# Five small moves in the RG-LRU stage of a hybrid streaming layer: the convolution's first tap, the fp16 hi halves, two buffer rings, and the place of the background work

## The chip, the cores and the metric

The kernel runs on one core of a Trainium2 chip. The metric is the device time of one execution in microseconds (us), the median of several runs. A core has five engines with a queue each: TensorE (PE, matmuls), VectorE (DVE), ScalarE (ACT), GpSimd (POOL) and SyncE (SP), which here issues nearly all DMAs. An engine runs its queue in order; semaphores order the engines against each other.

## The reference, cut to what matters

One layer is applied to 2048 prompt positions and to 32 sample positions (with cached keys and values of 512 positions). Both go through the same code, cut here to the path that the change touches:

```
z = rms_norm(x, norm_g) @ w_in                 # 1024 -> 6 x 512
xl, gl, q, k, v, ga = split(z)
xc = conv_b + sum(xl[t-3+k] * conv_w[k] for k in 0..3)      # causal, per channel
r  = sigmoid(xc @ gate_a_w + gate_a_b)         # 8 blocks of 64x64
i  = sigmoid(xc @ gate_x_w + gate_x_b)
a  = exp(-8 * r * softplus(-lambda))
h  = scan(h*a + sqrt(1-a*a) * (i*xc))          # over positions
lru = h * silu(gl)
att = banded attention of q, k, v * silu(ga)   # with the cache for the sample
h  = x + [lru, att] @ w_out
y  = h + (p @ w_pe) * sigmoid(rms_norm(h) @ w_pg)
```

The matmuls take fp16 pairs: each operand is scaled by a power of two and split into a hi half (rounded to fp16) and a lo half (the rest), and three of the four products are summed. The scale comes from a bound on the operand, the largest absolute value.

## The kernel before, in words

The kernel has a front part (about the first 640 us) and an attention part. In the front part the weights `w_in` are loaded and split, `proj(i, b)` (line 265 and on) computes one 128-row tile of q, k, v or the attention gate with 24 matmuls of 128x512, and `POST[b](i)` turns it into fp16 halves in DRAM. The RG-LRU path works on chunks of 256 positions: `l_proj(c, g)` (lines 575 to 616) computes 128 channels of `xl` and `gl` of chunk `c` with 48 matmuls of 128x256 (line 587). After them ACT writes `xl` (L600) and a sigmoid (L603), POOL makes the first tap of the convolution with its bias (L611), and DVE adds the other three taps (L614). `l_split` (lines 618 to 627) makes the halves `X`: ACT the two hi halves of 64 partitions each (L624), DVE the two lo halves (L625). `l_gates(c, g)` runs four small matmuls on `X` (L641) into one of two PSUM buffers of the pool `ps_g`, and ACT reads them with four sigmoids (L644, L645), which frees the buffer. `l_tail(c)` holds the exponentials, the square root and the scan, `l_halves(c)` the bound and the halves of the result.

`l_steps(c)` is a generator that yields between these calls. The loop (`for c in range(2, NCH - 2)`, line 810 and on) has a block per `proj`: a block takes two steps of `l_steps(c - 1)`, a `proj`, one step of the chunk before, and three or four steps of `background()`. A chunk has eight blocks; in the first four stands an `l_proj`. The background does what is not bound to a position: the bias rows (`ext_row`, `ext_store`), the cached keys and values, and the loading, bounding and splitting of `w_out`, `w_ple_gate` and `w_ple_proj` for the attention part. Its `pause` entries are steps that do nothing, between the loads of an operand and its bound. What is left of it after the loop is run at once after four more blocks (`for _ in bg: pass`).

A bound is a maximum over all partitions, `all_max` (lines 82 to 91): DVE puts each partition's maximum on the diagonal of `dg` (L87, one buffer), a matmul with ones spreads it (L90), and DVE reduces it (L91). This bound product takes a buffer of the same pool `ps_g` as the gates, and it is held behind the last matmul that was written down before it:

```
ps = ps_g.tile([128, 2, CW], F32, tag="g", name="psm").rearrange("p a b -> p (a b)")[:, :128]
with tc.issue_after(after.ins) if after else nullcontext():
    nc.tensor.matmul(ps, lhsT=ones, rhs=dg, start=True, stop=True)
```

The order of each engine's queue is set before the run by a planner that takes, of the instructions that are ready by its own estimate of time, the one written first. An instruction without such a hold can so stand in its queue ahead of work that is written before it.

`split(hi, lo, src, s)` (lines 155 to 163) makes the hi half on POOL (L158) or ACT (L160) and the lo half on DVE (L163). `v_half` (lines 406 to 412) splits 128 rows of the cached v into the tile `vTo`, which has one buffer and serves also `post_v` (lines 318 to 327), the v of the prompt (stored by L327). The tile `hlA` is a ring of two, used by the background's weights. `split` of the tokens is in `prep_x(i)` (L223 on ACT, then POOL and DVE, then the transposing DMA L234). `load_x`/`prep_x(SAMPLE)` stand in the first block of the chunk loop with `c == SP` (3), the four sample projections in its blocks 4 to 7.

Of the kernel before, what the change touches and what calls it, by code (L numbers as in the profile page):

```python
# [8 lines left out]
F32 = mybir.dt.float32  # L9
F16 = mybir.dt.float16  # L10
BF16 = mybir.dt.bfloat16
U32 = mybir.dt.uint32
AF = mybir.ActivationFunctionType
OP = mybir.AluOpType
# [20 lines left out]
def hybrid_layer(  # L35
# [313 lines left out]
    def background():  # L349
# [55 lines left out]

        def v_half(j, d):
            def f(st):
                t = Tp("vTo", [128, 2, 512], F16, 1)
                split(t[:, 0], t[:, 1], st[:, d], sV)
                nc.sync.dma_start(kc_d[2 * j + d][:, 1], t.rearrange("p a b -> p (a b)"))  # L410
            return f
# [51 lines left out]
        def load(st, src):  # L463
            nc.sync.dma_start(flat(st) if len(src.shape) == 2 else st, src)

        pause = [(None, ())] * 4
        items = [(None, (ext_load,))] + pause + [(None, (ext_row,))] + pause
        for src, factors, half in ((cache_k, k_factors, k_half), (cache_v, v_factors, v_half)):
            items += [(cache(src, j), (part_max(j),)) for j in range(2)] + pause
# [105 lines left out]
    def l_proj(c, g):  # L575
        n = width(c)
        pt = ps_x.tile([128, 2, CW], F32, tag="x", name="psx")
        for j in range(2):
            i = 0
            for k in range(8):  # L580
                for a, e in ((0, 0), (0, 1), (1, 0)):
                    if c == SAMPLE:
                        rhs, o = xT_s[:, e * 8 + k], pt[:, j, :n]
                    else:
                        rhs = xT[c][:, :, e * 8 + k, :]
                        o = pt[:, j].rearrange("p (a b) -> p a b", a=2)
                    m = nc.tensor.matmul(o, lhsT=wl[j][:, k, a, g * 128:(g + 1) * 128], rhs=rhs, start=i == 0, stop=i == 23)  # L587
                    i += 1
        last_mm[:] = [m]
        if g == 0:  # L590
            b = "s" if c == SAMPLE else ""
            C[c] = {k: TL(k + b, [128, 4, n if b else CW], F32, nb) for k, nb in (("i4", 1 if b else 2), ("sl4", 1 if b else 2))}
        xl = TL("xl", [128, CW + 3])
        if c == 0:
            nc.vector.memset(xl[:, 0:3], 0.0)
        elif c == SAMPLE:
            nc.vector.tensor_copy(xl[:, 0:3], col[:, SCV + 3 * g:SCV + 3 * g + 3])
        else:
            nc.vector.tensor_copy(xl[:, 0:3], hist[g])
        nc.scalar.activation(xl[:, 3:3 + n], pt[:, 0, :n], AF.Copy, scale=u_xl)  # L600
        z = C[c]["sl4"][:, g, :n]
        zs = TL("zs", [128, CW])[:, :n]
        nc.scalar.activation(zs, pt[:, 1, :n], AF.Sigmoid, scale=u_gl)  # L603
        nc.vector.scalar_tensor_tensor(z, pt[:, 1, :n], u_gl, zs, op0=OP.mult, op1=OP.mult)
        hb = small[:, (16 if c == SAMPLE else 0) + 3 * g:][:, :3] if c in (SAMPLE, NCH - 1) else \
            sm.tile([128, 3], F32, tag=f"hist{g}", name=f"hist{g}")
        nc.vector.tensor_copy(hb, xl[:, n:n + 3])
        if c != SAMPLE:
            hist[g] = hb
        xc = C[c]["i4"][:, g, :n]  # L610
        nc.gpsimd.tensor_scalar(xc, xl[:, 0:n], col[:, CWT + g:CWT + g + 1], col[:, CB + g:CB + g + 1],  # L611
                                op0=OP.mult, op1=OP.add)
        for k in range(1, 4):
            nc.vector.scalar_tensor_tensor(xc, xl[:, k:k + n], col[:, CWT + 4 * k + g:CWT + 4 * k + g + 1],  # L614
                                           xc, op0=OP.mult, op1=OP.add)
        l_split(c, g)

    def l_split(c, g):
        n = width(c)
        xc = C[c]["i4"][:, g, :n]  # L620
        X = TL("Xs", [128, 2, NS], F16, 4) if c == SAMPLE else TL("X", [128, 2, CW], F16, 4)
        for o in range(2):
            q, w = slice(o * 64, o * 64 + 64), slice((1 - o) * 64, (2 - o) * 64)
            nc.scalar.activation(X[q, o, :n], xc[q], AF.Copy, scale=sx[q, g:g + 1])  # L624
            nc.vector.scalar_tensor_tensor(X[w, o, :n], xc[q], sx[q, g:g + 1], X[q, o, :n], op0=OP.mult,  # L625
                                           op1=OP.subtract)
        xs_l[c, g] = X
# [154 lines left out]
    prep_w_in(3, stg[3])  # L782
    es_lt.close()
    lt.append(pool("lt", stack=esl))
    ls = l_steps(0)
    for i, b in ((3, 2), (0, 3), (1, 3), (2, 3), (3, 3)):
        next(ls)
        proj(i, b)
        next(ls)
    lp = None  # L790


    bg = background()

    def x_pair(n, c):

# [13 lines left out]
    for c in range(2, NCH - 2):  # L810
        steps = [(i, b) for i in (2 * c, 2 * c + 1) for b in (1, 0, 2, 3)]
        lp, ls = ls, l_steps(c - 1)
        for n, (i, b) in enumerate(steps):
            next(ls, None)
            proj(i, b)
            next(ls, None)
            next(lp, None)
            if c == 2:
                next(lp, None)
            for _ in range(4 if n % 3 == 0 else 3):  # L820
                next(bg, None)
            if c == SP and n == 0:
                load_x(SAMPLE)
                prep_x(SAMPLE)
            if c == SP and 4 <= n < 8:
                proj(SAMPLE, (1, 0, 2, 3)[n - 4])
            if c == SP + 1:
                next(lss, None)
                next(lss, None)
            x_pair(n, c + 1)  # L830
    c = NCH - 2

    def dense(lp, ls, steps):
# [467 lines left out]
```

## Time and profile before

| | before |
|---|---|
| median of 3 runs | 1241.63 us (1239.91 to 1242.02) |
| profiled execution: its own time / its span | 1243.85 us / 1241.9 us |
| PE busy | 1083.4 us (87%) |
| DVE / ACT / POOL busy | 828.2 (67%) / 609.7 (49%) / 451.0 us (36%) |
| mean granted TensorE clock | 0.943 of full |

The span runs from the first to the last instruction of the profiled execution. Busy time of PE is that of matmuls, whose ends are modelled. In a timeline row, the bracket at the end is the time for which the engine sat idle before the instruction, and what ended it.

### The profile page before, as it was taken

The page shows a single profiled execution, that of the slowest core. Times are in us where ns is not written, and L with a number is a line of the kernel's source. Part 1 is how long each engine was busy: PE and PEld are TensorE (multiplying, and loading weights), DVE is VectorE, ACT ScalarE, POOL GpSimd, SP SyncE. Part 2 cuts the span into 40 slices and gives each one's busy share as a digit, 9 for nine tenths or more (in the row PEclk, how much of TensorE's full clock was granted, in tenths as well). Part 3 has the DMA queues.
Part 4 walks back from the last instruction along what each step waited for, and adds up shares of the span by engine and source line. Part 5 has one row for each costly group of instructions (what it writes and reads, how often), then busy time and mean ns, then how long its engine had stood idle before and what let it go on. Part 6 is the DMA issues. An engine that isn't in the chain of part 4 may idle for free. (4 is left out here: it accounts for less than half of the span.)

```text
span 1241.9 us, 22414 instructions
## 1 busy us (share of the span) xinstructions
PE 1083.4 (87%) x8395; PEld 628.6 (51%) x8395; DVE 828.2 (67%) x1860; ACT 609.7 (49%) x1076; POOL 451.0 (36%) x518
## 2 busy tenths in 40 slices
PE   3779998976799789877988689999999999999896
PEld 1335664643465546555634445555555555555443
DVE  5986455844967756776855676667776776676544
ACT  6532565536557755448654254444444444444223
POOL 2875124424546334563420222222222222222221
PEclk9889999997899899978988699999999999999998
DMA  8775313689386684640598988899989899999841
GB/s 290 212 194 170 81 59 73 173 235 269 95 234 164 192 225 149 195 127 26 151 341 269 217 152 163 183 186 198 199 183 183 189 188 186 181 189 187 189 82 26
DMA packets 357725, 217.47 MB, mean 175 GB/s; under 512 B 296032, under 2 KB 298632, under 8 KB 357488
## 3 DMA queue, kind: packets, MB, share of 16 engines
q1 hardware_dynamic: 357184, 215.50, 71.9%
q8 instruction: 65, 1.06, 0.4%
q10 hardware_dynamic: 432, 0.54, 0.1%
q14 instruction: 44, 0.36, 0.1%
HBM read 98.87 MB, written 46.76 MB: 117 GB/s over the span
## 5 line engine op out<-in xcount | busy, mean ns | idle before, releaser
L183 PE MATMUL psp<-wA,xT 128*128 128x512 f16 x1536 | 363.5, 396 | 22.3 <-DVE t L308 9.4
L183 PEld LDWEIGHTS <-xT 128*128 128x128 f16 x1536 | 154.2, 101 | 237.7 <-issue 62.3
L994 ACT ACTIVATE S<-S,nb,s 128x640 f32<-128x640 f32 (+5 forms) x130 | 110.5, 850 | 222.9 <-DVE nb L991 214.4
L183 PE MATMUL psg<-g,hT 128*128 128x512 f16 (+1 forms) x792 | 180.8, 377 | 3.2 <-DVE gt L189 1.5
L587 PE MATMUL psx<-xT,wl 128*128 128x256 f16 x1536 | 181.2, 279 | 0.0
L587 PEld LDWEIGHTS <-wl 128*128 128x128 f16 x1728 | 158.8, 100 | 38.1 <-issue 13.3
L1010 DVE TENSOR_TENSOR Phl<-S,Phl 128x640 f16<-128x640 f32 (+4 forms) x126 | 97.8, 780 | 89.9 <-POOL Phl L1007 48.0
L1032 PE MATMUL pso<-kv,PT 128*128 128x64 f16 (+1 forms) x1704 | 117.1, 195 | 29.0 <-DVE att L1068 16.2
L1032 PEld LDWEIGHTS <-PT 128*128 128x128 f16 (+2 forms) x1800 | 109.7, 99 | 52.1 <-issue 21.4
L1007 POOL TENSOR_SCALAR Phl<-S 128x640 f16<-128x640 f32 (+4 forms) x63 | 48.6, 771 | 211.9 <-ACT S L994 171.3
L977 PE MATMUL pss<-kv,qT 128*128 128x128 f16 (+2 forms) x1200 | 108.1, 223 | 9.1 <-DVE mx L988 7.5
L183 PEld LDWEIGHTS <-hT 128*128 128x128 f16 x792 | 73.9, 99 | 79.5 <-issue 4.3
L977 PEld LDWEIGHTS <-qT 128*128 128x128 f16 (+1 forms) x1200 | 94.8, 100 | 21.2 <-issue 8.2
L988 DVE CUSTOM_DVE_ANT_0 S<-pss,bias 128x640 f32<-128x640 f32 (+4 forms) x128 | 92.9, 731 | 4.5 <-PE pss L977 4.0
L183 PE MATMUL psu<-o,AT 128*128 128x512 f16 x384 | 90.6, 387 | 0.9 <-DMA AT<-An 0.7
L183 PE MATMUL psu<-o,L 128*128 128x512 f16 x384 | 90.4, 386 | 0.2 <-DVE ga L337 0.2
L624 ACT ACTIVATE X<-i,sx 64x256 f16<-64x256 f32 x64 | 32.2, 504 | 75.9 <-DVE i L614 75.1
L1148 POOL TENSOR_TENSOR gt<-gt,h 128x512 f32<-128x512 f32 (+1 forms) x32 | 41.7, 1304 | 65.6 <-DVE gt L1147 58.5
L90 PE MATMUL psm<-dg,ones 128*128 128x128 bf16 x25 | 6.0, 239 | 66.8 <-DVE dg L87 37.5
L96 POOL TENSOR_TENSOR fh<-fh,pw 128x8 f32<-128x8 f32 (+1 forms) x34 | 58.5, 1721 | 2.2
L95 POOL TENSOR_SCALAR fh<-ssqh,e 128x8 f32<-128x8 f32 (+1 forms) x34 | 17.4, 511 | 112.3 <-DVE ssqh L282 79.1
L183 PEld LDWEIGHTS <-AT 128*128 128x128 f16 x384 | 36.4, 100 | 42.4 <-issue 4.6
(284 smaller groups left out, 1716.4 us busy)
## 6 DMA issues: line engine op xcount, KB each, us to landing
stw<-in_w_in_dram SPq DMA_DIRECT2D x20, 512.0 KB, 6.4
x<-in_x_prompt_dram SPq DMA_DIRECT2D x16, 512.0 KB, 4.4
stg<-in_w_out_dram SPq DMA_DIRECT2D x16, 512.0 KB, 5.1
stg<-in_w_ple_gate_dram SPq DMA_DIRECT2D x16, 512.0 KB, 4.6
qT<-qd SPq DMA_DIRECT2D x32, 256.0 KB, 5.5
kv<-kvd SPq DMA_DIRECT2D x16, 512.0 KB, 4.3
h<-in_x_prompt_dram SPq DMA_DIRECT2D x16, 512.0 KB, 4.9
out_dram<-gt SPq DMA_DIRECT2D x31, 256.0 KB, 2.3
```

Source lines behind the costliest of these rows:

```text
L95: nc.gpsimd.tensor_scalar(dst, ssq, mul, add, op0=OP.mult, op1=OP.add)
L96: nc.gpsimd.tensor_tensor(dst, dst, pw[:R, :n], op=OP.pow)
L183: m = nc.tensor.matmul(ps[:R], lhsT=l(a), rhs=r(e), start=first and j == 0, stop=last and j == 2)
L587: m = nc.tensor.matmul(o, lhsT=wl[j][:, k, a, g * 128:(g + 1) * 128], rhs=rhs, start=i == 0, stop=i == 23)
L624: nc.scalar.activation(X[q, o, :n], xc[q], AF.Copy, scale=sx[q, g:g + 1])
L977: last_mm[0] = nc.tensor.matmul(ps[rw, c], lhsT=q[:, h % 2, a * 4 + h // 2, :R], rhs=k[:, h, :n], start=a == 0, stop=a == 1)
L988: nc.vector.tensor_tensor_reduce(out=S[:, c0:c0 + W], in0=ps[:, c0:c0 + W], in1=bias[:, h, 640 - W:], op0=OP.add, op1=OP.max, scale=1.0, s ...
L994: nc.scalar.activation(S[:, c0:c0 + W], S[:, c0:c0 + W], AF.Exp, bias=nb[:, j:j + 1], scale=scP, accum_out=sums[i][:, e:e + 1])
L1007: nc.gpsimd.tensor_scalar(v[:, 0, :W], P[:, :W], 1.0, 1.0, op0=OP.mult, op1=OP.mult)
L1010: nc.vector.tensor_tensor(v[:, 1, :W], P[:, :W], v[:, 0, :W], op=OP.subtract)
L1032: nc.tensor.matmul(o[rw, o0:o0 + HD], lhsT=t[:n, a * (WP // 128) + c0 // 128 + j, rw], rhs=v[:n, e, h * HD:h * HD + HD], start=first and m ...
L1148: (nc.vector if end else nc.gpsimd).tensor_tensor(gt[:R], gt[:R], s["h"][:R, c], op=OP.add)
```

## The change

The first tap moves from POOL to ACT, the two hi halves of `X` from ACT to DVE. `xl` gets a second buffer, `X` has three in place of four. The cached v is split in the ring `hlA`. The background starts in the five blocks of chunk 0 with four steps each; in the chunk loop a block takes four steps, and three in blocks 0 and 4 (before: three, and four in blocks 0, 3 and 6). Each pause has six steps in place of four. The sample's load and `prep_x` stand in the last block of the chunk loop before, and its projections in blocks 1, 3, 5 and 7.

```diff
         def v_half(j, d):
             def f(st):
-                t = Tp("vTo", [128, 2, 512], F16, 1)
+                t = Tp("hlA", [128, 2, 512], F16, 2)
                 split(t[:, 0], t[:, 1], st[:, d], sV)
...
-        pause = [(None, ())] * 4
+        pause = [(None, ())] * 6
...
-        xl = TL("xl", [128, CW + 3])
+        xl = TL("xl", [128, CW + 3], F32, 2)
...
-        nc.gpsimd.tensor_scalar(xc, xl[:, 0:n], col[:, CWT + g:CWT + g + 1], col[:, CB + g:CB + g + 1],
-                                op0=OP.mult, op1=OP.add)
+        nc.scalar.activation(xc, xl[:, 0:n], AF.Identity, scale=col[:, CWT + g:CWT + g + 1],
+                             bias=col[:, CB + g:CB + g + 1])
...
-        X = TL("Xs", [128, 2, NS], F16, 4) if c == SAMPLE else TL("X", [128, 2, CW], F16, 4)
+        X = TL("Xs", [128, 2, NS], F16, 4) if c == SAMPLE else TL("X", [128, 2, CW], F16, 3)
...
-            nc.scalar.activation(X[q, o, :n], xc[q], AF.Copy, scale=sx[q, g:g + 1])
+            nc.vector.tensor_scalar(X[q, o, :n], xc[q], sx[q, g:g + 1], None, op0=OP.mult)
...
-    ls = l_steps(0)
+    ls, bg = l_steps(0), background()
     for i, b in ((3, 2), (0, 3), (1, 3), (2, 3), (3, 3)):
         next(ls)
         proj(i, b)
         next(ls)
+        for _ in range(4):
+            next(bg)
     lp = None
-
-    bg = background()
...
-            for _ in range(4 if n % 3 == 0 else 3):
+            for _ in range(4 if n % 4 else 3):
                 next(bg, None)
-            if c == SP and n == 0:
-                load_x(SAMPLE)
-                prep_x(SAMPLE)
-            if c == SP and 4 <= n < 8:
-                proj(SAMPLE, (1, 0, 2, 3)[n - 4])
+            if c == SP and n % 2:
+                proj(SAMPLE, (1, 0, 2, 3)[n // 2])
             if c == SP + 1:
                 next(lss, None)
                 next(lss, None)
             x_pair(n, c + 1)
+            if c == SP - 1 and n == 7:
+                load_x(SAMPLE)
+                prep_x(SAMPLE)
```

## Rows read from the trace of the kernel before

**Rows 1.** Busy time of the engines in two stretches; then granted clock, DMA share, GB/s.
```profile
93.00:205.00 112.00, 112.00 (x715) 69.65 (x714) 65.55 (x140) 54.53 (x92) 39.80 (x44) 1.00 0.37 99
205.00:640.00 435.00, 372.12 (x2490) 228.18 (x2489) 293.98 (x573) 250.42 (x430) 204.58 (x225) 0.92 0.63 176
```
**Rows 2.** Groups of matmuls, 205 to 640 us: busy, mean ns, idle before, releasers.
```profile
L183 PE MATMUL psp<-wA,xT 128*128 128x512 f16 x919 | 215.5, 393 | 5.7 <-DVE t L189 3.9 <-DVE t L308 1.8
L587 PE MATMUL psx<-xT,wl 128*128 128x256 f16 x1152 | 137.6, 281 | 0.0
L641 PE MATMUL psg<-X,gw 128*128 128x256 f16 x50 | 12.7, 278 | 10.9 <-DVE X L625 10.7
L181 PE MATMUL psp<-wA,xT_s 128*32 128x512 f16 x96 | 11.2, 496 | 5.1 <-DVE vTo L322 5.1
L90 PE MATMUL psm<-dg,ones 128*128 128x128 bf16 x15 | 3.6, 240 | 41.2 <-ACT ig L645 26.0 <-DVE dg L87 15.2
```
**Rows 3.** Timeline of PE, two blocks at full speed, then the longest waits.
```profile
238.88 5.34 PE L183 MATMUL psp<-wA,xT 128*128 128x512 f16 x24
244.06 5.40 PE L587 MATMUL psx<-xT,wl 128*128 128x256 f16 x48
249.30 5.34 PE L183 MATMUL psp<-wA,xT 128*128 128x512 f16 x24
...
286.70 0.27 PE L90 MATMUL psm<-dg,ones 128*128 128x128 bf16 x1 [14.82 <-ACT ig L645]
...
426.00 0.26 PE L90 MATMUL psm<-dg,ones 128*128 128x128 bf16 x1 [6.37 <-DVE dg L87]
...
461.87 0.27 PE L90 MATMUL psm<-dg,ones 128*128 128x128 bf16 x1 [4.99 <-ACT ig L645]
...
526.89 0.27 PE L90 MATMUL psm<-dg,ones 128*128 128x128 bf16 x1 [6.03 <-ACT ig L645]
...
538.11 0.27 PE L90 MATMUL psm<-dg,ones 128*128 128x128 bf16 x1 [5.82 <-DVE dg L87]
...
587.29 0.39 PE L641 MATMUL psg<-X,gw 128*128 128x256 f16 x1 [6.83 <-DVE X L625]
```
**Rows 4.** Timelines of SP, POOL and ACT on the way to the wait at 286.7 us.
```profile
269.45 0.45 SPq L327 DMA_DIRECT2D kvd<-vTo  x1
...
275.25 0.69 POOL L158 TENSOR_SCALAR vTo<-stg,sV 128x512 f16<-128x512 f32 x1 [5.97 <-DMA kvd<-vTo]
275.91 1.07 POOL L611 TENSOR_SCALAR i<-xl,col 128x256 f32<-128x256 f32 x1
...
278.85 1.04 ACT L624 ACTIVATE X<-i,sx 64x256 f16<-64x256 f32 x2 [9.52 <-DVE i L614]
...
286.09 0.56 ACT L645 ACTIVATE ig<-psg,bxs,ug 64x256 f32<-64x256 f32 x1
```
**Rows 5.** Timelines of ACT and DVE on the way to the wait at 538.1 us.
```profile
534.43 1.06 ACT L223 ACTIVATE xn<-x 128x1024 f16<-128x1024 f32 x1 [3.01 <-DMA xT<-xn]
...
536.01 1.01 DVE L625 SCALAR_TENSOR_TENSOR X<-i,sx,X 64x256 f16<-64x256 f32 x2 [2.47 <-ACT X L624]
```
**Rows 6.** Timeline of SP, early: a store of the background.
```profile
94.23 0.29 SPq L453 DMA_DIRECT2D row_d<-stg  x1
```
**Rows 7.** Groups by line and shape, whole span: prices of the instructions moved.
```profile
L611 POOL TENSOR_SCALAR i<-xl,col 128x256 f32<-128x256 f32 x32 | 24.1, 753 | 36.5 <-ACT xl L600 23.0 <-DVE X L625 8.9 <-DVE m L135 2.3
...
L624 ACT ACTIVATE X<-i,sx 64x256 f16<-64x256 f32 x64 | 32.2, 504 | 75.9 <-DVE i L614 75.1
...
L625 DVE SCALAR_TENSOR_TENSOR X<-i,sx,X 64x256 f16<-64x256 f32 x64 | 31.3, 489 | 11.7 <-ACT X L624 9.9
...
L336 DVE TENSOR_SCALAR t<-t,u_g 128x512 f32<-128x512 f32 x3 | 1.6, 540 | 0.0
```
**Rows 8.** Line L614 on DVE: duration ns min/median/max, first and last start.
```profile
L614 DVE SCALAR_TENSOR_TENSOR i<-xl,col,i x96: 455/484/1479, 123.4 to 624.8; 128x256 f32<-128x256 f32 x96
```
**Rows 9.** Busy time of the engines in the stretch 310.5 to 341.5 us, columns as rows 1.
```profile
310.50:341.50 31.00, 22.42 (x202) 13.08 (x202) 27.92 (x54) 15.96 (x27) 17.12 (x16) 0.87 0.36 95
```
## The prediction

> **What bounds the kernel now.** I first read the windows, to find the stretch that the change can touch. From 93 to 205 us PE is busy without a gap and its granted clock is 1.00; from 205 to 640 us it is busy for 372.12 of 435.00 us at a mean clock of 0.92 [rows 1]. So the second stretch has 62.9 us in which PE stands still, and no other engine is full in it: DVE has 293.98 us (68%), ACT 250.42, POOL 204.58. The attention part behind it has no line of the change.
>
> The groups of matmuls say what ended these gaps: 41.2 us stand before the bound products, 26.0 of them ended by the gates' sigmoid on ACT that frees the PSUM buffer and 15.2 by `dg` on DVE; 10.9 us before the gates' own matmuls, for `X`; 5.7 and 5.1 us before projections whose results DVE had not yet taken up, all three in the stretch of the sample's projections [rows 2]. That is the whole: 62.9 us.
>
> A gap costs more than itself. At the full clock a projection and an `l_proj` together take 10.42 us from start to start, 5.18 and 5.24 [rows 3]. 919 and 1152 such matmuls [rows 2] are 919/24 x 5.18 = 198.4 and 1152/48 x 5.24 = 125.8 us; for the other 419 small ones I estimate 24 us. That makes 348 us where 372 were busy: 24 us went to matmuls behind a gap, at the lower of the two clocks. Each us of gap removed is so worth 1 + 24/62.9 = 1.38 us, and all of it together 87 us.
>
> Then I followed the longest waits back by the timelines of the other engines. **The wait of 14.82 us at 286.7 us** [rows 3]: the store of the prompt's `vTo`, issued at 269.45, frees the only buffer 5.8 us later; POOL has the cached v's hi half at the head of its queue and waits 5.97 us for it, with the first tap behind it; the hi halves of `X` on ACT wait 9.52 us for the convolution, with the sigmoids behind them, which end at 286.65 and free the PSUM buffer [rows 4]. **The wait of 5.82 us at 538.1 us**: ACT stands for 3.01 us at `xn` until a transposing DMA is through, its hi halves of `X` come after that, DVE waits 2.47 us for them at its lo halves, and `dg` is behind those in DVE's queue [rows 5]. In both, an `X` half that hops between engines passes on a delay from elsewhere.
>
> **The change, part by part.**
>
> *First tap to ACT.* POOL loses 32 instructions of 0.753 us, 24.1 us [rows 7], and the sample's four short ones. ACT gains 32 of about 0.50 us (the 256-element copy L624, 0.504 [rows 7]), 16 us; it comes right behind `xl`, its input, on the same engine, so it adds no wait. Nothing waits longer than this half microsecond, and the covered ACT has 185 us free in the stretch.
>
> *Hi halves to DVE.* ACT loses 64 of 0.504 us, 32.2 us, and 75.1 us of waiting for the convolution [rows 7], in which the sigmoids stood in line. DVE gains 64 instructions, for which no row stands. L336, the same form at twice the length, takes 0.540, so half of it, 0.27, is the lower end; the lo half L625, which reads two tensors, 0.489 [rows 7]. I take 0.35, nearer to the row of the same form: 22 us, of which 56/64, 20 us, fall behind 205 us. The upper end for one that meets POOL is the longest of L614, 1.479 [rows 8].
>
> *Cached v in the ring.* The same four splits and stores, but the wait of 5.97 us on the prompt's store goes; at the worst they wait for an earlier pair of the ring, and POOL no longer holds a tap.
>
> *Background and pauses.* Counted in steps, the bound products of `cache_k`, `cache_v` and the four 512-column weight jobs stood in blocks 4, 8, 14, 20, 25 and 30 of the chunk loop and now stand in 0, 4, 10, 16, 21 and 26; that of `w_ple_proj` moves from the rest that is run at once into block 31, and of 18 left-over steps 4 remain. With the pauses alone they would have come later; the 20 steps in chunk 0 outweigh them. Work without a hold runs ahead already: the bias row's store, written in the chunk loop, is issued at 94.23 us, ahead of the first `l_proj` [rows 6]. So it is the held products, and what follows from them (halves, the stores and loads of the bias rows), that moves some 30 us forward, part of it into the stretch with a DMA share of 0.37 [rows 1]. The DMAs are the same in number; SP's queue has them beside other transposes.
>
> *The sample* alternates with the prompt instead of standing in four blocks on end. *`xl`* doubled lets ACT write ahead of the taps; *`X`* with three buffers still covers the two groups of lag and the one being written. I cost both at nothing.
>
> **The sum.** Gaps that go, in us: 14.8 (both its causes go); 5.8 at 538 (`X` no longer asks ACT); 3.0, the rest of the 15.2 for `dg`, a product of the cached keys that now comes earlier; 4.5 of the 6.0 at 526.9, whose sigmoids were behind `X` and stand in the crowded rest; half of the 6.4 at 426 (a weight's bound, whose loads have two more steps); half of the sample's 10.8; 2.4 of the 10.9 for `X`. Together 39.1, times 1.38 is 54 us. I leave standing the 4.99 us at 461.9, a transpose again, and the 6.83 at 587.3, where DVE itself is late [rows 3].
>
> What is late next is DVE. Its share in the stretch goes from 68% to (294 + 20)/(435 - 40) = 79%. Where it is now at 27.92 of 31.00 us, PE stands for 8.6 us of that window [rows 9], and 10.8 with the part of its first gap that lies before it (5.1 and 5.7 [rows 2]). I take one such window more, 10.8 x 1.38 = 15 us. The forecast is 54 - 15 = 39 us off the profiled execution's own 1243.85, 1205. That execution is 2.2 us above the median of the runs, so **1202.6 us**.
>
> **The rivals.**
>
> *A, nothing takes the gaps' place.* The halves counted above go whole and DVE causes no new gap: 62.9 - 8.2 (587 and the small one for `X`) - 5.0 = 49.7, times 1.38 is 69 us, 1173 us. For it: PE had no gap at all from 93 to 205 us. Against: there DVE was at 59% [rows 1].
>
> *B, the work only changes its place.* The held products come earlier, but the stores and loads of the bias rows now meet the transposes of the next tokens, and new gaps open behind these, as at 461.9 us. With 45 us of the 54 given back it stays at 9 us: 1233 us.
>
> *C, slower: DVE becomes the bound.* Each hi half that meets POOL waits for it. The place is the pair of `X` halves in every `l_proj` block; the price is up to 1.479 - 0.35 = 1.1 us a half beyond the sum [rows 8], 56 x 1.1 = 62 us, and DVE is then at 294 + 20 + 62 = 376 of 435 us, 86%, close to the window of rows 9. If five of the stretch's fourteen windows of 31 us were like that one, they would cost 5 x 10.8 x 1.38 = 75 us against the 54 gained: 21 us slower, 1262 us. It decides from the point at which four windows are so (54/14.9 = 3.6). Against it: the median of L614 is 0.484, so few meet POOL [rows 8], and POOL loses 24 us.
> [...]
>
> *D, the early start does nothing,* because the work ran ahead anyway [rows 6]. Then the 3.0, the 4.5 and the 3.2 us are not gained: 10.7 x 1.38 = 15 us less, 1218 us. This is inside the forecast's own range.
>
> **How the numbers follow.** The forecast with D, 1190 to 1220: 0.52. A, 1173 to 1190: 0.19. B, 1220 to 1244: 0.18, of which 0.12 is faster by more than 0.2%. C: 0.11. A measurement of this kernel can tell about 0.2%, 2.5 us, from no change. Faster: 0.52 + 0.19 + 0.12 = 0.83. Within: 0.05. Slower: 0.12, C and the end of B. For 8 in 10 the range leaves out C, the last of B and the last of A: 1175 to 1237 us.
>
> **What would show it.** Right: no wait of POOL for a `vTo` store; no wait of ACT for L614 at the hi halves; DVE's hi halves near 0.35 us and DVE near 310 us in what is left of the stretch; idle time before the bound products down from 41.2 to about 15 us; the granted clock in the stretch above 0.95; the bound products of the cache before 205 us. Wrong, if the gaps before bound products stand as they are with another releaser (the gates were late for a reason that I missed), if hi halves on DVE take over 1 us, or if projections wait for DVE in every chunk.

## The result and the profile after

The changed kernel takes **1232.43 us** (median of 6 runs, 1230.57 to 1235.33) where the kernel before took 1241.83 us (6 runs, 1236.95 to 1245.65): ratio 0.9939, 95% interval [0.9919, 0.9959]. (The ratios in this text are those on record, estimated from all runs, and not quotients of the two medians, which here would be 0.9924.) It is faster, and inside the range, but the gain is 8 to 9 us and not 39. A second timing of the same kernel, in the experiments below, gives 0.9955 [0.9934, 0.9977].

| | after |
|---|---|
| profiled execution: its own time / its span | 1231.86 us / 1229.9 us |
| PE busy | 1078.4 us (88%) |
| DVE / ACT / POOL busy | 850.8 (69%) / 591.3 (48%) / 430.5 us (35%) |
| mean granted TensorE clock | 0.947 of full |

First the windows of [rows 1], in the changed kernel:
```profile
93.00:205.00 112.00, 109.12 (x702) 68.39 (x700) 71.79 (x157) 48.61 (x80) 33.59 (x33) 1.00 0.39 105
205.00:640.00 435.00, 375.22 (x2505) 229.07 (x2505) 309.67 (x616) 238.68 (x405) 189.85 (x202) 0.93 0.63 176
```
The work has changed engines as meant: DVE has 15.7 us more in the second stretch, ACT 11.7 and POOL 14.7 less. PE stands still for 59.8 us there and for 2.9 before 205 us, together 62.7 us. Before, it was 62.9. So the sum of the gaps has hardly moved.

A window with fixed ends holds more work when the work comes earlier. So I also took the windows from 0 to the first reciprocal of the attention part (L1067), at 680.4 us before and 675.1 after. Of the kernel before:
```profile
0.00:680.40 680.40, 569.27 (x3581) 336.21 (x3582) 454.65 (x961) 368.98 (x644) 305.19 (x340) 0.93 0.63 178
```
and of the one after:
```profile
0.00:675.10 675.10, 567.82 (x3580) 334.57 (x3581) 478.03 (x1038) 351.22 (x610) 284.35 (x305) 0.93 0.63 179
```
The same matmuls are done 5.3 us sooner: 3.9 us less idle time (111.1 and 107.3) and 1.5 us less of matmuls. The profiled executions differ by 12.0 us in their spans. The other 6.7 us lie behind it, in the attention part, in which no line was changed; more of that below.

The groups of matmuls, 205 to 640 us, that answer to [rows 2]:
```profile
L183 PE MATMUL psp<-wA,xT 128*128 128x512 f16 x935 | 222.9, 398 | 15.2 <-ACT sq L656 9.9 <-DVE vTo L322 2.5 <-DVE t L308 1.2
L587 PE MATMUL psx<-xT,wl 128*128 128x256 f16 x1152 | 135.1, 278 | 0.0
L641 PE MATMUL psg<-X,gw 128*128 128x256 f16 x50 | 12.9, 282 | 16.0 <-DVE X L625 8.3 <-ACT ig L645 7.8
L181 PE MATMUL psp<-wA,xT_s 128*32 128x512 f16 x96 | 7.6, 380 | 1.2 <-DVE m L135 1.2
L90 PE MATMUL psm<-dg,ones 128*128 128x128 bf16 x14 | 3.4, 245 | 29.2 <-ACT ig L645 22.3 <-DVE dg L87 6.8
```
And the waits of [rows 3], in the timeline of PE:
```profile
209.85 0.26 PE L90 MATMUL psm<-dg,ones 128*128 128x128 bf16 x1 [7.74 <-ACT ig L645]
...
292.80 0.27 PE L90 MATMUL psm<-dg,ones 128*128 128x128 bf16 x1 [5.80 <-ACT ig L645]
318.40 6.92 PE L183 MATMUL psp<-wA,xT 128*128 128x512 f16 x24 [9.86 <-ACT sq L656]
...
389.87 0.37 PE L641 MATMUL psg<-X,gw 128*128 128x256 f16 x1 [6.67 <-ACT ig L645]
...
466.39 0.26 PE L90 MATMUL psm<-dg,ones 128*128 128x128 bf16 x1 [3.65 <-ACT ig L645]
502.57 0.27 PE L90 MATMUL psm<-dg,ones 128*128 128x128 bf16 x1 [6.16 <-DVE dg L87]
539.00 0.22 PE L90 MATMUL psm<-dg,ones 128*128 128x128 bf16 x1 [0.66 <-DVE dg L87]
...
585.42 0.37 PE L641 MATMUL psg<-X,gw 128*128 128x256 f16 x1 [5.67 <-DVE X L625]
```
Which bound a product belongs to is told by the reduction that follows it on DVE (`mbL` a chunk's result, `ma` a weight, `cka` the cache). Sorted in this way, 93 to 640 us, in us:

| PE waits before | before | after |
|---|---|---|
| bounds of the chunks' results | 25.8 | 10.6 |
| bounds of the background (cache, weights) | 15.4 | 18.6 |
| the gates' products | 10.9 | 16.0 |
| projections | 10.8 | 16.4 |

So the moves did what they were to do: 15.2 us went from the chunks' bounds. 14.0 us came in the three other rows. (The sum after is 1.1 us short of 62.7, the start of a wait before a projection that reaches beyond 640 us.)

**Why they came back** is seen for the most part on ACT. Its longest waits, 93 to 640 us (engine, line, what it waited for: us in total, times, longest), before:
```profile
ACT X L624 <- DVE i L614: 75.1, 25, 9.5
ACT qN L312 <- DVE t L308: 29.4, 10, 5.3
...
ACT xn L223 <- DMA xT<-xn: 16.5, 4, 10.2
ACT xn L223 <- DMA x<-in_x_prompt_dram: 8.7, 3, 5.5
```
and after:
```profile
ACT qN L312 <- DVE t L308: 43.8, 9, 8.2
ACT xn L223 <- DMA xT<-xn: 29.1, 6, 9.7
ACT xn L223 <- DMA x<-in_x_prompt_dram: 23.0, 5, 7.6
...
ACT xn L223 <- DMA x<-in_x_sample_dram: 6.0, 1, 6.0
```
The wait for the convolution is gone. But ACT now arrives earlier at the next tokens' square (L223). That line writes into `xn`, which has one buffer, held until the transposing DMA of the tokens before has read it, and reads `x`, which has one buffer as well. ACT's wait there goes from 28.2 us (with the sample's 3.0) to 58.1, and the sigmoids are still queued behind. Its wait for the scaled queries of DVE (L308) grows too, from 29.4 to 43.8 us. The timelines of DVE, SP and ACT ahead of the 5.80 us at 292.8:
```profile
251.54 1.28 DVE L163 SCALAR_TENSOR_TENSOR xn<-x,rs,xn 128x1024 f16<-128x1024 f32 x1 [0.97 <-POOL xn L158]
...
283.67 0.38 SPq L302 DMA_DIRECT2D kvds<-kTo  x1
284.14 3.00 SPq L234 DMA_TRANSPOSE xT<-xn  x1
...
278.56 0.58 ACT L611 ACTIVATE i<-xl,col 128x256 f32<-128x256 f32 x1
288.86 1.06 ACT L223 ACTIVATE xn<-x 128x1024 f16<-128x1024 f32 x1 [9.71 <-DMA xT<-xn]
...
290.48 0.55 ACT L644 ACTIVATE r<-psg,col,ug 64x256 f32<-64x256 f32 x1
...
292.19 0.56 ACT L645 ACTIVATE ig<-psg,bxs,ug 64x256 f32<-64x256 f32 x1
```
The DMA that it waits for is issued by SP at 284.14 and takes 4.7 us to land. What it reads was complete at 252.82, 31.3 us earlier. In SP's queue it stands behind the store L302, which SP could issue only when another transposing DMA, of the prompt's keys, had landed at 283.65. So its place in that queue makes it late; how much earlier the tile `xT` that it writes, a ring of two, would have been free for it, no run here separates. It is the picture of [rows 4] with another wait at its head. The waits at 389.9 and 466.4 us have a square in front of them too, that stood for 6.54 and 5.81 us. These three make 16.1 of PE's 62.7 us; the rest has other causes. Before the 7.74 us at 209.85 ACT stood for 4.33 us at a hi half of the cached keys (L390), until their transposing DMA landed at 203.99; before the 4.05 us at 455.3 (not in the rows above) it stood for 3.61 us at L312.

The new 9.86 us at 318.4 us, before a projection, come at least in part from the background. The row names L656 on ACT, but that instruction does not touch `psp` and ended at 318.40, when the projection started. The last reader of a `psp` before that is L291 on DVE, which ended at 318.34; the variant with the hi halves on ACT, further down, has a wait of 7.46 us in the same place, and there the row names L291. DVE's own queue, and the busy time of the engines in this wait and in the window of [rows 9]:
```profile
309.87 2.33 DVE L163 SCALAR_TENSOR_TENSOR hlA<-stg,sg,hlA 128x512 f16<-128x512 f32 x1 [1.79 <-POOL hlA L158]
312.13 1.22 DVE L652 TENSOR_TENSOR r<-r,cl 128x1024 f32<-128x1024 f32 x1
...
317.66 0.68 DVE L291 TENSOR_TENSOR t<-psp,fh 128x512 f32<-128x512 f32 x1
...
309.87:318.40 8.53, 0.00 (x1) 0.01 (x1) 8.53 (x7) 4.08 (x5) 8.53 (x7) 0.59 0.55 153
310.50:341.50 31.00, 19.95 (x142) 10.21 (x143) 28.18 (x45) 20.82 (x33) 13.83 (x11) 0.83 0.74 212
```
From 309.87 to 318.40 DVE and POOL are busy without a gap, and halves of `w_out` (`hlA`) stand ahead of L652 and L291. The halves of the weights now begin at 295.1 us, where they began at 331.8 before.

Finally the new instructions (ns min/median/max, first and last start):
```profile
L624 DVE TENSOR_SCALAR X<-i,sx x64: 326/353/1265, 123.9 to 624.4; 64x256 f16<-64x256 f32 x64
...
L611 ACT ACTIVATE i<-xl,col x32: 583/595/605, 121.7 to 621.5; 128x256 f32<-128x256 f32 x32
```

### The profile page after: what moved, and what is told of

It is laid out like the page before. It is cut to its first block, busy times and chain, and to the rows that moved or that the text cites. A ratio compares the mean times of both kernels' runs of the same rounds, so it can differ in the third digit from the quotient of the medians.

```text
span 1229.9 us, 22389 instructions
## 1 busy us (share of the span) xinstructions
PE 1078.4 (88%) x8395; PEld 626.2 (51%) x8395; DVE 850.8 (69%) x1932; ACT 591.3 (48%) x1040; POOL 430.5 (35%) x482
## 5 line engine op out<-in xcount | busy, mean ns | idle before, releaser
L183 PE MATMUL psp<-wA,xT 128*128 128x512 f16 x1536 | 368.3, 400 | 30.1 <-ACT sq L656 9.9
L587 PE MATMUL psx<-xT,wl 128*128 128x256 f16 x1536 | 178.7, 276 | 0.0
L95 POOL TENSOR_SCALAR fh<-ssqh,e 128x8 f32<-128x8 f32 (+1 forms) x34 | 17.5, 514 | 126.4 <-DVE ssqh L282 99.8
L96 POOL TENSOR_TENSOR fh<-fh,pw 128x8 f32<-128x8 f32 (+1 forms) x34 | 61.0, 1793 | 1.6
L183 PEld LDWEIGHTS <-L 128*128 128x128 f16 x384 | 35.6, 98 | 38.5
```

The lines of the kernel that those rows point to most:

```text
L95: nc.gpsimd.tensor_scalar(dst, ssq, mul, add, op0=OP.mult, op1=OP.add)
L96: nc.gpsimd.tensor_tensor(dst, dst, pw[:R, :n], op=OP.pow)
L183: m = nc.tensor.matmul(ps[:R], lhsT=l(a), rhs=r(e), start=first and j == 0, stop=last and j == 2)
```

## The experiments

The theory is that the gaps are handed on: each part takes a wait out of ACT's or POOL's queue, and the engine then stands at the next thing that is late, above all at the square whose buffers the token DMAs hold. The rivals are that the PSUM buffers of the gates are the limit, that the burst of bias-row loads and stores on SP is what the token DMAs wait behind, and that the gain was given back by one of the moved parts alone.

**The change in parts.** First the kernel before once more:

> The kernel before, unchanged, for a second trace. Of the 12.0 us between the two profiled spans only 2.3 us are there at the last gates of the front part; most of the rest arises in the attention part, where the order of PE's last 8897 instructions is the same. If that part differs by chance from execution to execution, this span lies some 4 us below the first one (about 1238), and the time from the third to the sixteenth of the attention tiles (reciprocal L1067 on VectorE) is nearer to 426 than to the 432 us of the first trace; if the change itself makes the attention part faster, that time is 432 again and the span 1242.

1242.43 us. Its gaps stand where they stood (14.84 us at 286.5), the first reciprocal is at 680.0 us, and the time from the third to the sixteenth reciprocal is 432.0 us again. The picture of before repeats.

The moves of work alone, on the kernel before:
```diff
-        xl = TL("xl", [128, CW + 3])
+        xl = TL("xl", [128, CW + 3], F32, 2)
...
-        nc.gpsimd.tensor_scalar(xc, xl[:, 0:n], col[:, CWT + g:CWT + g + 1], col[:, CB + g:CB + g + 1],
-                                op0=OP.mult, op1=OP.add)
+        nc.scalar.activation(xc, xl[:, 0:n], AF.Identity, scale=col[:, CWT + g:CWT + g + 1],
+                             bias=col[:, CB + g:CB + g + 1])
...
-        X = TL("Xs", [128, 2, NS], F16, 4) if c == SAMPLE else TL("X", [128, 2, CW], F16, 4)
+        X = TL("Xs", [128, 2, NS], F16, 4) if c == SAMPLE else TL("X", [128, 2, CW], F16, 3)
...
-            nc.scalar.activation(X[q, o, :n], xc[q], AF.Copy, scale=sx[q, g:g + 1])
+            nc.vector.tensor_scalar(X[q, o, :n], xc[q], sx[q, g:g + 1], None, op0=OP.mult)
```

> The kernel before with the engine moves alone: first tap on ScalarE, hi halves on VectorE, xl twice and X three times buffered; background, pauses, sample and the cached v as before. Theory T (the moves only uncover the next thing that ScalarE's queue waits for, the square of the tokens, whose target xn is held by the transposing DMA): a few us at most, ratio 0.995 to 1.000, idle time before bound products about 35 us, with ScalarE's wait for DMA xT<-xn above the 16.5 us of before. Rival (my sum): the gaps at 538 and 526 go, ratio about 0.985.

1.0047 [1.0031, 1.0064]: 0.5% slower, clear of noise, which neither theory had expected. In the waits of ACT the square has taken the place of `X`:
```profile
ACT xn L223 <- DMA xT<-xn: 42.7, 6, 14.6
```

The ring alone:
```diff
-                t = Tp("vTo", [128, 2, 512], F16, 1)
+                t = Tp("hlA", [128, 2, 512], F16, 2)
```

> The kernel before with the cached v split in the halves' ring and nothing else. My sum: the wait of 14.8 us before the bound product of chunk 1 goes, with 1.38 us per us, ratio 0.984. Theory T: the same transposes hold ScalarE's xn at that point (2.87 us are on record there), so half of it stays: ratio 0.990 to 0.996.

1.0028 [1.0013, 1.0042]: slower too, again outside both ranges, though the wait of 14.82 us is gone. PE and ACT in its place:
```profile
290.78 0.37 PE L641 MATMUL psg<-X,gw 128*128 128x256 f16 x1 [7.84 <-DVE mbL L91]
...
283.63 1.06 ACT L223 ACTIVATE xn<-x 128x1024 f16<-128x1024 f32 x1 [9.55 <-DMA xT<-xn]
```
The store was the first of two waits in a row. With it removed, ACT stands 9.55 us at the square and then 3.40 us at the load of a weight, PE 7.84 us behind both, and PE's idle time to the first reciprocal is 113.9 us where it was 111.1.

The order alone (the pauses, the start in chunk 0, the steps per block, the sample's places):
```diff
-        pause = [(None, ())] * 4
+        pause = [(None, ())] * 6
...
+        for _ in range(4):
+            next(bg)
...
-            for _ in range(4 if n % 3 == 0 else 3):
+            for _ in range(4 if n % 4 else 3):
...
-            if c == SP and n == 0:
-                load_x(SAMPLE)
-                prep_x(SAMPLE)
-            if c == SP and 4 <= n < 8:
-                proj(SAMPLE, (1, 0, 2, 3)[n - 4])
+            if c == SP and n % 2:
+                proj(SAMPLE, (1, 0, 2, 3)[n // 2])
...
+            if c == SP - 1 and n == 7:
+                load_x(SAMPLE)
+                prep_x(SAMPLE)
```

> The kernel before with the order alone: background from chunk 0 on, six pauses, four steps a block, the sample's places; engines, buffers and the cached v as before. My sum: some 15 to 20 us (3.0 + 4.5 + 3.2 + 5.4 us of gaps at 1.38), ratio 0.985. Theory T: the stores and loads of the bias rows meet other transposes, gaps move and do not go, ratio 0.997 to 1.005.

0.9963 [0.9948, 0.9978], between my sum and the theory's range, and nearer to the latter. The next run is of this same kernel, and not of the one that its expectation speaks of:

> The kernel before with the background's part of the order alone (from chunk 0 on, six pauses, four steps a block) and the sample where it was. My sum had 7.4 us for the sample and 15 for the bound products. If the background makes the gain of order_only (0.9963), this is 0.994 to 0.998; if the sample's places make it, 0.999 to 1.003.

So this run says nothing on the sample; as a repeat it gives 0.9966 [0.9944, 0.9988]. The kernel that was meant has the first three of these edits, and the sample where it was before:


> What the run order_nosample was to be and was not (it ran the kernel of order_only a second time): the kernel before with the background's part of the order alone, the sample's load and projections where they were. If the background makes the gain of order_only (0.9963 and 0.9966), this is 0.994 to 0.998; if the sample's places make it, 0.999 to 1.003.

0.9924 [0.9900, 0.9949]. And the whole change with the sample's three places put back:

> The changed kernel with the sample's load, split and projections where they were before. If the sample's new places cost what the two runs of the order alone and of its background part differ by (0.9963 against 0.9924, 0.4%), and that cost adds, this is near 0.990, 1227 us. Rival: the cost does not add, because the moves of the engines already change what stands beside the sample; then it is at the changed kernel's 0.994 to 0.9955, or slower.

0.9907 [0.9882, 0.9932], against 0.9939 and 0.9955 of the whole change. Both pairs say that the sample's new places cost some 0.3 to 0.5%; the intervals of the pairs overlap, touch or barely part, so this is likely and not proved.

**The whole with one move undone.** The hi halves back on ACT, and then the first tap back on POOL (the diffs are those above, reversed):

> The changed kernel with the hi halves back on ScalarE (the first tap stays there). Theory T (in the new order ScalarE is late anyway by the tokens' path, so the moved halves are worth little): ratio to before 0.994 to 1.000, within 0.3% of the changed kernel. My sum had the halves' move as the cause of some 10 us: ratio 1.000 to 1.006.

0.9963 [0.9942, 0.9984], and on ACT the old wait stands again, with the square's wait halved:
```profile
ACT X L624 <- DVE i L614: 55.2, 23, 6.8
...
ACT xn L223 <- DMA xT<-xn: 13.8, 5, 5.6
```
Within the whole change the halves' move takes 55 us of waiting off ACT and brings no time that shows.

> The changed kernel with the first tap back on GpSimd. Theory T: within 0.3% of the changed kernel, 0.993 to 0.998. My sum (a tap behind GpSimd's queue holds ScalarE no more, as the hi halves are on VectorE; but VectorE waits for it): 0.998 to 1.004.

1.0032 [1.0013, 1.0051], 0.8 to 0.9% over the whole change: within the new order the tap's move is worth more than that of the halves or of the sample (the ring and the background's order were not undone within the whole). The theory had expected no more than 0.3%. PE's idle time to the first reciprocal is 114.9 us against 107.3, spread over many waits, and the reciprocal comes at 683.7 us. Since the moves together are slower on the kernel before, the parts do not add: by themselves they multiply to 1.0047 x 1.0028 x 0.9963 = 1.0038, and the whole is 0.9939.

**The square's buffers.** The square needs only its sum, so its values can go to a scratch tile, and the square no longer waits for `xn`:
```diff
-        nc.scalar.activation(xn[:R, 0], x[:R], AF.Square, scale=2.0 ** -8, accum_out=ssq[:R])
+        junk = Tp("hlA", [128, D], BF16, 2)
+        nc.scalar.activation(junk[:R], x[:R], AF.Square, scale=2.0 ** -8, accum_out=ssq[:R])
```
On the kernel before, on the moves alone and on the whole change, the last beside a second timing of the whole change:

> The kernel before with the same scratch tile for the square of the tokens. There ScalarE waited 16.5 us for DMA xT<-xn, and 75 us for the convolution. Theory T: a smaller gain than on the changed kernel, since the hi halves of X keep ScalarE late anyway: ratio 0.990 to 0.998. If the gain is as large here as on the changed kernel, the moved halves have nothing to do with it.

> The engine moves alone on the kernel before (measured 1.0047), plus the scratch tile for the square of the tokens, so that ScalarE waits for no transposing DMA. Theory T (the moves lost because ScalarE, freed of waiting for the convolution, stands 42.7 us at xn with the gates behind it): the loss is gone, ratio 0.993 to 0.999. If ScalarE's wait at xn is not what the moves lost by, it stays at 1.003 to 1.006.

> The changed kernel once more, timed and with a second trace. Ratio to before 0.992 to 0.996. If the 6 us by which its attention part was shorter belong to this program, the stretch from the seventh to the sixteenth attention tile is 292 us again (298 in both traces of before); if they were chance it lies between 294 and 299.

> The changed kernel with the square of the tokens (L223 on ScalarE) written to a scratch tile of the ring hlA in place of xn, so that ScalarE no longer waits for the transposing DMA of the tokens before. Theory T (that wait, 29.1 us in 6 times, is what now makes the gates late): the gaps at 293, 390 and 466 us go (16.1 us), ratio to before 0.975 to 0.983, no wait of ScalarE for DMA xT<-xn. Rival R1 (GpSimd's hi half of the tokens then waits for the same DMA and holds the norms behind it): the gaps come back before projections, ratio 0.990 to 0.998.

0.9999 [0.9979, 1.0019] on the kernel before, where ACT stood little at the square; 0.9975 [0.9952, 0.9999] on the moves, which had 1.0047; 0.9920 [0.9892, 0.9948] on the whole, which had 0.9955 beside it. So the edit is worth 0.7% on the moves, nothing on the kernel before, and 0.2 to 0.4% on the whole, where the intervals overlap and 0.975 to 0.983 had been expected. The times are in line with the theory, but only the moves are clear of noise, and the traces show that little idle time is saved. Windows to the first reciprocal, the moves alone:
```profile
0.00:690.00 690.00, 574.38 (x3582) 337.00 (x3583) 480.20 (x1038) 349.76 (x610) 278.57 (x305) 0.92 0.62 175
```
and with the scratch tile:
```profile
0.00:680.60 680.60, 561.84 (x3578) 333.89 (x3579) 475.53 (x1038) 348.82 (x609) 273.11 (x305) 0.93 0.63 177
```
PE's idle time has even grown, from 115.6 to 118.8 us, as ACT now stands at a weight's load instead (18.8 us, and PE 21.94 us behind it). What fell is the time of the matmuls, by 12.5 us. In the whole change the three waits of PE behind the square, 5.80, 6.67 and 3.65 us, do shrink, to 2.31 us in the second place and nothing in the others: so the square was their cause. But the time went elsewhere, and PE's idle time to the first reciprocal fell only from 107.3 to 103.8 us. The sample's load is issued late, and PE, ACT and SP show (the edit adds a line, so that L224 is the square and L235 the tokens' DMA)
```profile
262.83 3.60 PE L181 MATMUL psp<-wA,xT_s 128*32 128x512 f16 x24 [16.42 <-DMA xT_s<-xn]
...
252.50 1.05 ACT L224 ACTIVATE hlA<-x 32x1024 bf16<-32x1024 f32 x1 [15.35 <-DMA x<-in_x_sample_dram]
...
236.84 6.37 SPq L235 DMA_TRANSPOSE xT<-xn  x1
...
246.47 0.47 SPq L216 DMA_DIRECT2D x<-in_x_sample_dram  x1
```
Between the last two, SP issues two stores of the front's results and three DMAs of the bias rows.

**The PSUM buffers.** The whole change with three buffers for the gates and bound products, two for `l_proj`:
```diff
-    ps_x = pool("ps_x", bufs=3, space=PSUM, stack=esl)
-    ps_g = pool("ps_g", bufs=2, space=PSUM, stack=esl)
+    ps_x = pool("ps_x", bufs=2, space=PSUM, stack=esl)
+    ps_g = pool("ps_g", bufs=3, space=PSUM, stack=esl)
```

> The changed kernel with three PSUM buffers for gates and bound products and two for the LRU projections, in place of two and three. Rival R2 (the bound products are late because they share two buffers with the gates): the 30 us of gaps that ScalarE's sigmoids ended go, ratio 0.970 to 0.980. Theory T: the sigmoids are as late as before and hold up what comes next, a third to a half of the 30 us goes, ratio 0.983 to 0.990. If two buffers are too few for the LRU projections, gaps appear before L587, which had none.

0.9956 [0.9935, 0.9977], as the whole change beside it, and above both expected ranges. Before bound products and gates PE's idle time does fall by half, from 45.2 to 22.9 us (93 to 640 us), so the two buffers were a cause of these waits. But it comes back before projections, 32.4 us where it was 17.5 in the same window (11.57 of them at 317.8), and 4.8 us stand before the matmuls of `l_proj`, which had none and have lost a buffer here. As an account of the total this rival falls; what three buffers would do without taking one from `l_proj` was not run.

**SP's burst.** The loads and stores of the eight bias rows, in one run before, are put between the halves of the weights:
```diff
-        for h in range(H):
-            items.append((bass.AP(tensor=row_d.tensor, offset=row_d.offset + 767 * h, ap=[[0, 128], [1, 767]]),
-                          (ext_store(h),)))
+        exts = [(bass.AP(tensor=row_d.tensor, offset=row_d.offset + 767 * h, ap=[[0, 128], [1, 767]]),
+                 (ext_store(h),)) for h in range(H)]
...
+            for j, (_, dst, k0) in enumerate(parts):
+                items += [(srcs[j], [w_half(dst, k0, k, gcol) for k in range(2)])]
+                if j % 2 and exts:
+                    items.append(exts.pop(0))
```
On the whole change, on it with the scratch tile, and on the kernel before:

> The changed kernel with the eight loads and stores of the bias rows spread, two to each of the first four weight jobs, in place of one after the other behind the cached v. Theory B (the tokens' loads and transposes meet this burst; that is where the gaps at 280 to 320 us come from, 18 us, and the waits of ScalarE for x): these gaps go at least by half, ratio to before 0.980 to 0.988. Rival (the transposes are slow in any case): ratio as the changed kernel, 0.994 to 0.998.

0.9880 [0.9851, 0.9909], 1222.75 us: faster than both kernels, at the edge of what theory B expected. ACT's waits at the square:
```profile
ACT xn L223 <- DMA xT<-xn: 25.0, 5, 11.6
ACT xn L223 <- DMA x<-in_x_prompt_dram: 9.4, 4, 4.4
```
The wait for the tokens' load falls from 23.0 to 9.4 us, the one for the transposing DMA hardly. The first reciprocal is at 666.1 us, with 3.6 us less idle time of PE and 5.4 us less of matmuls than in the changed kernel.

> Both: scratch tile and spread bias rows, on the changed kernel. In the scratch version a gap of 16.4 us stands at 263 us, behind a load of the sample's tokens that SyncE issued late among the bias rows. Theory B: that gap goes or falls under 5 us, ratio to before 0.970 to 0.982. Rival: another gap of its size appears, ratio 0.990 to 0.995.

0.9897 [0.9871, 0.9923]: the scratch tile adds nothing on top, as the rival had it.

> The kernel before with the bias rows spread over the weight jobs and nothing else. Theory B (the burst of the bias rows holds up the tokens' loads and transposes and the store of the prompt's v): the 14.8 us wait at 286.7 us goes here too, with no other part of the change, ratio 0.985 to 0.992. If the burst matters only once the background is earlier, 0.997 to 1.002.

1.0094 [1.0074, 1.0114]: on the kernel before it is a loss, which neither expectation had, and its longest wait stays (the edit moves what follows by two lines; L647 is the sigmoid L645):
```profile
286.27 0.27 PE L90 MATMUL psm<-dg,ones 128*128 128x128 bf16 x1 [14.00 <-ACT ig L647]
```
So the burst was not what the kernel before waited for; it became a cost in the new order. Why the spreading costs 0.9% there, I did not find.

Last, what the experiments point to: the rows spread, and the sample where it was before.

> The changed kernel with the bias rows spread over the weight jobs, and with the sample where it was before. If the two gains add, it is near 0.988 - 0.004 = 0.984, 1219 us, faster than any kernel so far. Rival: each edit only moves the waits, and it stands at 0.988 or above.

0.9886 [0.9860, 0.9912]. It does not beat the spread alone; the 0.3 to 0.5% of the sample's places do not add here.

All that bears on the front part in one view (the first reciprocal, and PE busy and idle until then, in us):

| kernel | ratio | first reciprocal | busy | idle |
|---|---|---|---|---|
| before | 1 | 680.4 | 569.3 | 111.1 |
| moves alone | 1.0047 | 690.0 | 574.4 | 115.6 |
| ring alone | 1.0028 | 682.5 | 568.6 | 113.9 |
| order alone | 0.9963 | 674.6 | 565.2 | 109.4 |
| order of the background alone | 0.9924 | 672.3 | 566.7 | 105.6 |
| whole change | 0.9939 | 675.1 | 567.8 | 107.3 |
| whole, tap on POOL | 1.0032 | 683.7 | 568.8 | 114.9 |
| whole, rows spread | 0.9880 | 666.1 | 562.4 | 103.7 |

## Why the prediction was wrong in size

The sign and the range were right, and the price of the hi halves; the sum was not. What came has the time of the rival B, "the work only changes its place" (1233 us), to which I gave 0.18. Its mechanism is borne out in part: the gaps were handed on, and spreading the bias rows gives some time back, but other gaps, at 209.85 and 318.4 us, opened without them. That its time is met within a microsecond is luck: its 45 us were chosen and not worked out, and only 5.3 of the 12.0 us between the profiled executions lie ahead of the attention part.

**The sum, the step that failed.** "Gaps that go" took seven terms one by one, each wait with the cause that the trace showed, and let nothing but one DVE window come in their place. The largest of them did shrink where they stood: the 14.82 became 5.80, the 5.82 became 0.66; the cached keys' product, with 2.98 before, now stands at 174.4 us without a wait. But the total hardly fell (62.9 and 62.7 us), since the queues had their next late thing close behind. [Rows 5] showed one: ACT stood for 3.01 us at `xn` *before* the halves. That gap did go, but the same wait now stands ahead of three others (16.1 us). I asked what the halves wait for, and not what ACT waits for next once it no longer waits for the halves. The ring alone shows this best: one wait of 14.82 us removed, 7.84 us behind the square and a weight's load in its place, and 2.8 us more idle time to the first reciprocal in all.

**What is late next.** I named DVE alone, with one window at 15 us. DVE has 309.67 us, near what I had worked out (294 + 20 = 314), and PE's waits for `X` went from 10.7 to 8.3 us, so it is not the bound of the whole stretch. But the crowded window of [rows 9], of which half the sample's 10.8 us was to go, stands: DVE has 28.18 of 31.00 us there (27.92 before), PE stands still for 11.05 us (8.6 before), and the 9.86 us, with DVE and POOL full, end in it. What the sum left out are the token DMAs with the single buffers of `xn` and `x` (16.1 us of PE's idle time), and the cached keys' transposes (7.74 us).

**The early start.** Right that the held work moves some 30 us forward: the bias rows' first load from 250.4 to 214.4, `w_out`'s halves from 331.8 to 295.1. Right in sign as well: the background's order is the only part that gains by itself (0.9924), so the rival D falls. But the step costed the DMAs at "the same in number; SP's queue has them beside other transposes", and the halves at nothing. They cost: they stand in DVE's queue ahead of the 9.86 us at 318.4, and spreading the rows gives back 0.6 to 0.8%. The cached values' product came to 209.85 us and not before 205, with 7.74 us of wait where it had none. The bound of `w_ple_proj`, in block 31, waits 6.16 us at 502.6, where I had 4.5 of 6.0 us gone at 526.9.

**The sample**, "alternates ... instead of standing in four blocks on end": half of its 10.8 us were to go. Before projections 16.4 us stand after, and by the runs the new places probably cost and do not gain.

**The first tap.** 0.595 us each and not 0.50: 3 us more on ACT. No wait of ACT stands before it. I gave only what it would cost; why it is worth 0.8 to 0.9% in the new order stays open.

**The hi halves.** 0.353 us in the median, where I took 0.35. Only two of the 64 take over 0.36: 1.265 us at 274.83, beside POOL's L294 and L296, and 0.696 at 623.68, beside POOL's L646. Five others that overlap an instruction of POOL take 0.333 to 0.354. So the rival C falls: not each that meets POOL waits for it. That some do, the kernel before shows as well: all 13 of the 96 L614 of [rows 8] that take over 0.5 us run beside an instruction of POOL (the 1.479 us at 508.01 beside L296 and L158), and the 79 beside which POOL is idle take 0.455 to 0.486. In the changed kernel other instructions are stretched too: in the window of the 9.86 us, with both engines full, POOL's hi half of the tokens (L158) takes 2.64 us where its median is 1.12, and DVE's lo half of a weight (L163) 2.33 where it is 0.75. Why an instruction of the one takes longer beside one of the other, no run here shows. ACT's 75.1 us of waiting went, as said, and bought nothing that shows (0.9963 with the halves back on ACT, 0.9939 and 0.9955 without).

**The factor of 1.38** for each us of gap is met by this pair of traces (3.9 us of idle time and 1.5 of matmuls), but by luck: in the second traces of the same two kernels it is 1.9 and 4.1 us, and the scratch tile on the moves raised the idle time by 3.2 us and cut the matmuls by 12.5. The time of the matmuls does not follow the idle time in proportion.

**The checks promised.** Right: no wait of POOL for a `vTo` store, no wait of ACT for L614 at the hi halves, L624 near 0.35, DVE near 310. Wrong: the idle time before bound products, 29.2 us and not 15; the granted clock, 0.93 and not above 0.95. Half right: the cache's bounds. The first sentence under "wrong" was the one to heed, if in another form: the gaps before bound products fell, but the total stands, with other waits at the head of the chains.

**What stays open.** Of the 12.0 us between the profiled spans, 6.7 lie behind the first reciprocal. From the seventh to the sixteenth of those reciprocals it is 298.4 and 298.2 us in two executions of the kernel before, 292.1 and 294.3 in two of the changed one, but also 299.2 and 295.9 in two executions of one and the same kernel, the order alone. How much of it belongs to the program is not settled; nor is why the parts interact as they do (the tap, the spreading on the kernel before).

## What to carry to other kernels

A wait at the end of a chain is worth what is left when the engine that carried it has gone on to the next instruction in its queue that is late (with the ring alone 14.82 us went, and 7.84 came in their place): before a gap is counted as gone, walk down that queue to the next wait for a DMA or for a tile with one buffer, and take the difference only. Sum the gaps by what PE was about to do, before and after; when the total stands still, look for the new releaser at the head of the old chain. And time the parts of a change both alone and left out of the whole: here moves that together are a loss in one order hold one that is worth 0.8% in the other. Last, check that a releaser that the profile names touches the tile that was waited for.

## What was not expected of the hardware

Issuing the tokens' transposing DMAs kept SP's queue for long and varying times, 1.43 to 8.90 us in the changed kernel, and their plain loads for 0.33 to 1.21 (ns min/median/max):
```profile
L234 SPq DMA_TRANSPOSE xT<-xn x16: 1429/1989/8902, 12.2 to 542.4; - x16
...
L216 SPq DMA_DIRECT2D x<-in_x_prompt_dram x16: 332/503/1210, 2.2 to 488.6; - x16
```
The longest, 8.90 us, stands at 26.45 us, ahead of the stretch; behind 205 us the longest is 5.65. SP's next DMA behind the 8.90 us starts at 35.41, 0.06 us after its end. In the variant with the scratch tile the next one behind the 6.37 us at 236.84 starts at 243.31, and the sample's load, with five DMAs before it, at 246.47. The prediction counted DMAs by their number alone.
